# A two-layer DiT-like network on one core: the rotary sine product as one VectorE instruction with reversed blocks, and the column sums of layer 1's mixer gate moved from the attention phase to the convolution phase

## The chip, the cores and the metric

The kernel runs on 1 core of one Trainium2 chip. The metric is the device time of one execution in microseconds (us), the median of several runs. The core's engines are TensorE (PE in the profile, with its weight loads as PEld), VectorE (DVE), ScalarE (ACT), GpSimd (POOL) and SyncE (SP), which here only issues transfers. Each engine executes its own instructions in the order in which they were queued, and waits for the other engines through semaphores.

## What is computed

The reference works on 512 tokens of width 1024 (`x`), 256 context tokens and one conditioning vector. Cut to what bears on the change:

```python
def ada_params(cond, w_ada, b_ada):
    m = jax.nn.silu(cond) @ w_ada + b_ada          # 1024 x 6144: six vectors of 1024
    return jnp.split(m[..., None, :], 6, axis=-1)

def apply_rope(x, cos, sin):                        # head dim 64: four blocks of 16
    x1, x2, x3, x4 = jnp.split(x, 4, axis=-1)
    rot = jnp.concatenate([-x2, x1, -x4, x3], axis=-1)
    return x * cos[None, :, None, None, :] + rot * sin[None, :, None, None, :]
...
for l in range(DEPTH):                              # 2 layers
    sh_m, sc_m, g_m, sh_f, sc_f, g_f = ada_params(c, ada_w[l], ada_b[l])
    h = modulate(x, norm_mix[l], sh_m, sc_m)
    y = even_mixer(...) if l % 2 == 0 else odd_mixer(...)
    x = x + g_m * y
    x = x + g_f * ec_moe(modulate(x, norm_ffn[l], sh_f, sc_f), ...)
```

Layer 0's mixer is differential attention: 6 heads, each with two query and two key vectors of 64 and a value of 128. Queries and keys are normalised by their root mean square, multiplied by a gain, and rotated. Layer 1's mixer is a gated short convolution, `(bg * shortconv(cg * u)) @ w_out`. After each mixer comes a mixture of 16 experts in which each expert takes its 64 best tokens. The mixer's gate `g_m` of layer 1 is one of the 12 adaptive vectors; it multiplies the output of the convolution mixer, and nothing needs it earlier.

## The kernel before

**Phases.** By the time of the profile: a prologue (0 to 60 us), the attention heads (60 to 340), the attention's output projection with the first router (340 to 445), the first MoE (445 to 925), the convolution mixer (925 to 1136), and the second MoE (1136 to 1640). A scheduler of the tile framework puts each engine's instructions into one in-order queue, by priorities and by its own estimate of when operands are ready. A change in one instruction can therefore move others.

**Matrix products** outside the MoE run as three fp32r matmuls on operands split into a high and a low part (`mm3`). So each operand costs a rounding copy (`split`, ScalarE, line 244) and a subtraction (VectorE, line 245).

**An attention head.** While head h's scores, softmax and value products run, the projections of head h+1 are made, one token tile of 128 at a time, over six tiles (four of tokens, two of context). `proj_fin` (lines 391 to 424) ends a token tile. Of the 256 columns `j m d` (j: query or key, m: which of the two, d: 64), ScalarE makes the squares (L396) and the value's high part; VectorE makes the value's low part, the product with the cosine table `cosg` (L401), the product of the block-swapped columns with the sine table `sing` (L409: four instructions of 128x64, one for each b and j), the sum of squares (L417) and the sum of both products (L421); GpSimd makes the inverse root (L81, L82) and the scaled result `qk` (L423). TensorE then transposes `qk` (`proj_tr`, L440). Only the four token tiles have the sine product, so it occurs 6 x 4 = 24 times. Of one score tile, VectorE takes the row maximum (L463), ScalarE the exponential (L464), VectorE the reciprocal and its product with lambda (L470, L471), ScalarE scales one half (L472), VectorE combines both halves into `p` (L473), and TensorE transposes `p` (L486); the split of the transposed `p` gives `ah` and `al`.

**The tables** (`tables`, lines 312 to 322) are made once in the prologue: cosine and sine multiplied by the gains.

**The adaptive vectors** that are not needed at once are made in the gaps of other phases. One vector w of layer l takes four parts: `ada_part` (lines 158 to 170) loads two rows of a 1 MB slab, ScalarE scales one (L164, 128x1024), VectorE multiplies and adds (L168, two instructions of 128x512), and, except for the first part, GpSimd accumulates (L170, two instructions of 128x512). After four parts `ada_sum` (L172 to L177) sums the accumulator over the partitions with 8 matmuls on a column of ones (16 passes in the trace, `tr<-ones,ada`) and VectorE adds the bias (L177). `ada_steps` (L179) spreads the parts over a number of calls: NSTEP = 21 in the attention for 28 parts (layer 0's vectors 2 to 5 and layer 1's 0 to LW-1, with LW = 3), and 11 in the convolution for 12 parts (layer 1's vectors LW to 5).

**The ring.** The slabs, the heads' weights, the convolution's weights (`cw`) and the output projections' weights (`wo`) share a ring of RA = 4 buffers of 1 MB. A load is issued on SP's queue (L148 for most), and waits there until a buffer is free; behind it wait all later loads.

**The output projections** (`OutProj`, from L675) multiply each weight tile by the gate's row: VectorE `wg` (L699), ScalarE `woh` (L706), GpSimd `wol` (L707), then the matmuls `pj<-woh,zh` and its two companions, and VectorE adds the result to x (L721). The gate's row is built from the adaptive vector 2 by `gate_row` (L209 to L219: 8 matmuls `tr<-ident,ada`, two ScalarE copies). In the attention phase the output projection's object is made during the last head but one; in the convolution after the second of four column groups (`cp == 1`, L1212), when its first half is also run.

## Time and profile before

| | us |
|---|---|
| median of 3 runs | 1639.68 (1635.38 to 1641.67) |
| the profiled execution | 1642.39 |
| its span, first to last instruction | 1640.6 |
| outside the span | 1.8 |
| TensorE busy in the span | 1523.1 (93%) |
| VectorE busy | 694.3 (42%) |
| ScalarE busy | 385.8 (24%) |
| GpSimd busy | 222.7 (14%) |
| mean granted clock of TensorE | 0.969 |

The durations below come from the one profiled execution, whose time stands 2.7 us above the median. The share of an engine over the whole span says little, because the phases have different loads: VectorE has 42% of the span, but far more of the attention phase. So each stage is read by itself: first how busy its engines are, then what TensorE waited for in it, then the timeline around the longest of these waits.

### The profile page before, as it was taken

To read this page: it belongs to the slowest core of one execution; us is meant where nothing else is said; L and a number is where in the kernel's file an instruction comes from. 1 tells how busy PE (TensorE), PEld (TensorE's weight loads), DVE (VectorE), ACT (ScalarE), POOL (GpSimd) and SP (SyncE) were. 2 spreads that over 40 slices of the span, in tenths; PEclk is the share of its full clock that TensorE was granted. 3 is DMA by queue.
4 is the path that set the end of the run, shared out by engine and by line. 5 is a ranking of instruction groups with operands and counts; after the bars stand their busy time and mean duration, and the time that the engine had idled before them with its cause. 6 is when DMAs were issued, how large, how long until landed. Compare 5 with 4: busy or idle time off the path is not lost. (4 is left out here: it accounts for less than half of the span.)

```text
span 1640.6 us, 20218 instructions
## 1 busy us (share of the span) xinstructions
PE 1523.1 (93%) x8052; PEld 908.4 (55%) x8052; DVE 694.3 (42%) x1470; ACT 385.8 (24%) x745; POOL 222.7 (14%) x237
## 2 busy tenths in 40 slices
PE   5999999989689999999999899997899999999998
PEld 1988888868434434443443487886544444344343
DVE  3878888886512122212212668544221221221222
ACT  4545555553111000100100443222110010001010
POOL 0344445652000000000000024311000000000000
PEclk9899999989799999999999999998899999999999
DMA  9433534564698999999999456448899999999994
GB/s 347 156 103 129 177 132 154 170 214 189 253 380 315 409 409 409 409 409 409 409 408 395 145 180 227 133 154 321 307 365 398 409 409 409 409 409 408 409 405 184
DMA packets 162779, 494.82 MB, mean 302 GB/s; under 512 B 11749, under 2 KB 42878, under 8 KB 161662
## 3 DMA queue, kind: packets, MB, share of 16 engines
q1 hardware_dynamic: 161600, 491.23, 78.3%
q10 hardware_dynamic: 1086, 2.31, 0.4%
q8 instruction: 63, 1.03, 0.3%
q14 instruction: 30, 0.25, 0.0%
HBM read 491.41 MB, written 2.10 MB: 301 GB/s over the span
## 5 line engine op out<-in xcount | busy, mean ns | idle before, releaser
L965 PE MATMUL s<-we,xs 128*64 128x512 f32 x2048 | 450.8, 595 | 4.0 <-DVE xs L940 4.0
L965 PEld LDWEIGHTS s<-we,xs 128*64 128x64 f32 x2048 | 142.7, 137 | 281.8 <-issue 272.3
L965 PE MATMUL pj<-we,aT 128*64 128x512 f32 x896 | 206.1, 602 | 0.0
L66 PEld LDWEIGHTS tr<-oh,x 128*128 128x128 f32 x1024 | 122.4, 196 | 52.7 <-issue 52.7
L66 PE MATMUL tr<-oh,x 128*128 128x128 f32 x1024 | 134.7, 286 | 2.2 <-DVE oh L913 2.2
L940 DVE TENSOR_SCALAR xs<-tr,am,ada 128x128 f32<-128x128 f32 x64 | 26.1, 408 | 252.6 <-PE tr L66 252.6
L1043 DVE TENSOR_TENSOR act<-act,s 128x512 f32<-128x512 f32 x32 | 20.6, 684 | 251.9 <-PE s L965 251.8
L965 PEld LDWEIGHTS pj<-we,aT 128*64 128x64 f32 x896 | 59.7, 137 | 104.6 <-issue 99.2
L993 DVE TENSOR_TENSOR x<-x,tr 128x512 f32<-128x512 f32 x64 | 43.6, 684 | 142.7 <-PE tr L66 142.7
L170 POOL TENSOR_TENSOR ada<-ada,adaw 128x512 f32<-128x512 f32 x60 | 85.7, 1439 | 108.3 <-DVE adaw L168 48.7
L938 ACT ACTIVATE xs<-tr,ada,am 128x128 f32<-128x128 f32 x64 | 29.3, 457 | 296.2 <-DVE xs L940 296.2
L66 PE MATMUL pj<-whi,hh 128*128 128x384 f32 (+1 forms) x256 | 85.0, 333 | 0.4 <-ACT whi L244 0.4
L66 PE MATMUL pj<-wlo,hh 128*128 128x384 f32 (+1 forms) x256 | 83.8, 327 | 0.0
L66 PE MATMUL pj<-whi,hl 128*128 128x384 f32 (+1 forms) x256 | 82.7, 323 | 0.0
L1053 ACT COPY aT<-s 128x512 f32<-128x512 f32 x32 | 18.7, 585 | 222.2 <-PE s L1052 222.2
L1158 POOL TENSOR_TENSOR crs<-xsq 128x4 f32<-128x4 f32 x1 | 0.2, 200 | 503.1 <-ACT xT L1125 503.1
L1037 ACT ACTIVATE act<-s 128x512 f32<-128x512 f32 x32 | 17.4, 594 | 206.1 <-PE s L965 206.1
L66 PE MATMUL pj<-chh,clo 128*128 128x512 f32 x160 | 62.1, 390 | 0.9 <-DVE clo L245 0.9
L66 PE MATMUL pj<-chh,chi 128*128 128x512 f32 x160 | 62.4, 390 | 0.0
L66 PE MATMUL pj<-chl,chi 128*128 128x512 f32 x160 | 62.1, 389 | 0.0
L168 DVE SCALAR_TENSOR_TENSOR adaw<-adaw,cin 128x512 f32<-128x512 f32 x60 | 51.1, 865 | 23.2 <-ACT adaw L164 23.2
L707 POOL TENSOR_TENSOR wol<-wg,woh 128x512 fp32r<-128x512 f32 x32 | 45.2, 1426 | 99.9 <-ACT woh L706 94.9
(312 smaller groups left out, 2374.9 us busy)
## 6 DMA issues: line engine op xcount, KB each, us to landing
we<-in_moe_w_gate_dram SPq DMA_DIRECT2D x128, 1024.0 KB, 13.5
we<-in_moe_w_up_dram SPq DMA_DIRECT2D x128, 1024.0 KB, 16.9
we<-in_moe_w_down_dram SPq DMA_DIRECT2D x124, 1024.0 KB, 14.3
adaw<-in_ada_w_dram SPq DMA_DIRECT2D x48, 1024.0 KB, 5.3
cw<-in_conv_w_in_dram SPq DMA_DIRECT2D x12, 1024.0 KB, 5.4
wqk<-in_attn_w_in_dram SPq DMA_DIRECT2D x10, 512.0 KB
wo<-in_attn_w_out_dram SPq DMA_DIRECT2D x4, 1024.0 KB
we<-in_moe_w_down_dram SPq DMA_DIRECT2D x8, 512.0 KB
```

The lines of the kernel that those rows point to most:

```text
L66: return T.matmul(o, l, r, start=start, stop=stop, skip_group_check=True)
L168: V.scalar_tensor_tensor(o, s[:, 0, cs], cin[:, 0, j:j + 1], s[:, 1, cs], op0=ALU.mult, op1=ALU.add)
L170: G.tensor_tensor(acc[:, cs], acc[:, cs], o, op=ALU.add)
L707: G.tensor_tensor(lo, wg, hi.bitcast(F32), op=ALU.subtract)
L938: A.activation(o_, i_, AF.Identity, bias=sh[:, kk:kk + 1], scale=am[:, kk:kk + 1])
L940: V.tensor_scalar(o_, i_, am[:, kk:kk + 1], sh[:, kk:kk + 1], op0=ALU.mult, op1=ALU.add)
L965: pe(T.matmul(acc[hf][64 * j:64 * j + 64, :], lhs[:, 2 * kk + k, 64 * j:64 * j + 64], ws[j][:, k, hf * 512:hf * 512 + 512], start=kk == 0 ...
L993: V.tensor_tensor(x1[tt][:, cs], src[tt][:, cs], b, op=ALU.add)
L1037: A.activation(act[:, hf * 512:hf * 512 + 512], ga[hf], AF.Silu)
L1043: V.tensor_tensor(act[:, cs], act[:, cs], up[hf], op=ALU.mult)
L1053: A.copy(aT[:, 4 * k4:4 * k4 + 4, :].rearrange("p k c -> p (k c)"), b[k4])
L1158: G.tensor_tensor(rs, xsq[:, :, 0], xsq[:, :, 1], op=ALU.add)
```

## The change

There are two edits, and a consequence of the first.

1. The sine product of `proj_fin` is one instruction of 128x256. Its input is read with the two 16-blocks of each pair in reversed order (`src[:, :, ::-1, :]`), and its table has one row for every one of the 256 columns.
2. For that, the table `sing` is stored for both m (twice the size), and the gains are first copied with their 16-blocks swapped (`gx`, four copies of 128x2x16). The eight table products of 128x4x16 become four of 128x4x64.
3. LW goes from 3 to 2: layer 1's vector 2, the gate of its mixer, is made in the convolution phase. The attention keeps 24 parts and 6 column sums over the same 21 steps; the convolution gets 16 parts and 4 sums over the same 11 steps.

```diff
-        sing = tabs.tile([128, NT, 2, 64], F32, name="sing")
+        sing = tabs.tile([128, NT, 2, 2, 64], F32, name="sing")
+        gx_ = tabs.tile([128, 2, 64], F32, name="gx")
...
+            for b in range(4):
+                V.tensor_copy(gx_[:, :, 16 * b:16 * b + 16], gb[:, :, 16 * (b ^ 1):16 * (b ^ 1) + 16])
...
-                for b in range(4):
-                    V.tensor_tensor(sing[:, :, j, 16 * b:16 * b + 16], sing[:, :, 1, 16 * b:16 * b + 16],
-                                    gj[:, None, 16 * (b ^ 1):16 * (b ^ 1) + 16].to_broadcast([128, NT, 16]),
-                                    op=ALU.mult)
+                for m in range(2):
+                    V.tensor_tensor(sing[:, :, j, m, :], sing[:, :, 1, 1, :],
+                                    gx_[:, j, None, :].to_broadcast([128, NT, 64]), op=ALU.mult)
...
-                src = p[:, :256].rearrange("p (j m u b i) -> p j m u b i", j=2, m=2, u=2, b=2)
-                dst = t2.rearrange("p (j m u b i) -> p j m u b i", j=2, m=2, u=2, b=2)
-                tb_ = sing[:, tt].rearrange("p j (u b i) -> p j u b i", u=2, b=2)
-                for b in range(2):
-                    for j in range(2):
-                        V.tensor_tensor(dst[:, j, :, :, b, :], src[:, j, :, :, 1 - b, :],
-                                        tb_[:, j, None, :, b, :].to_broadcast([128, 2, 2, 16]),
-                                        op=ALU.mult)
+                src = p[:, :256].rearrange("p (g b i) -> p g b i", b=2, i=16)
+                V.tensor_tensor(t2.rearrange("p (g b i) -> p g b i", b=2, i=16), src[:, :, ::-1, :],
+                                sing[:, tt].rearrange("p j m (u b i) -> p (j m u) b i", u=2, b=2), op=ALU.mult)
...
-LW = 3
+LW = 2
```

What this does to the queues is shown at three places. The line numbers of the changed kernel differ by 2 or 3 (L699 is its L696, L396 its L398); `x2` behind a row means two instructions in a row.

The first is ScalarE's queue in head 0 (`adaw` is a slab being scaled; `p,su` an exponential; `qsq`, `qv`, `qk`, `ah` the steps of a tile's end and of the splits). Before:

```order
L464 ACTIVATE p,su<-s_902,nm 128x768
L464 ACTIVATE p,su<-s_903,nm 128x768
L396 ACTIVATE qsq<-pj 128x256
L244 CAST qv<-pj 128x128
L472 ACTIVATE p<-p,rc 128x768
L396 ACTIVATE qsq<-pj 128x256
L244 CAST qv<-pj 128x128
L164 ACTIVATE adaw<-adaw,cin 128x1024
L244 CAST qk<-tr 128x256
L244 CAST ah<-tr 128x3x128
L464 ACTIVATE p,su<-s_1041,nm 128x768
```

The same stretch in the changed kernel:

```order
L461 ACTIVATE p,su<-s_888,nm 128x768
L164 ACTIVATE adaw<-adaw,cin 128x1024
L461 ACTIVATE p,su<-s_889,nm 128x768
L398 ACTIVATE qsq<-pj 128x256
L244 CAST qv<-pj 128x128
L469 ACTIVATE p<-p,rc 128x768
L398 ACTIVATE qsq<-pj 128x256
L244 CAST qv<-pj 128x128
L244 CAST qk<-tr 128x256
L244 CAST ah<-tr 128x3x128
L461 ACTIVATE p,su<-s_1021,nm 128x768
```

The slab's scaling has moved from ahead of the split `qk` to between the two exponentials.

The second is the start of the last head, VectorE (`rc` is the softmax's reciprocal and its product, `amc` a modulation row that the convolution needs, `wg` the gated output weight). Before:

```order
L417 TENSOR_REDUCE qss<-qsq 128x2
L177 TENSOR_TENSOR ada_82<-tr,pcol 128x8
L168 SCALAR_TENSOR_TENSOR ada<-adaw,cin 128x512 x2
L470 RECIPROCAL rc<-su 128x2
L168 SCALAR_TENSOR_TENSOR adaw<-adaw,cin 128x512
L471 TENSOR_TENSOR rc<-rc,lam 128x1
L238 SCALAR_TENSOR_TENSOR amc<-ada_82,pcol 128x8
L699 TENSOR_TENSOR wg<-wo,gate_3643 128x512 x2
L473 SCALAR_TENSOR_TENSOR p<-p,rc 128x768
```

The same in the changed kernel:

```order
L414 TENSOR_REDUCE qss<-qsq 128x2
L467 RECIPROCAL rc<-su 128x2
L468 TENSOR_TENSOR rc<-rc,lam 128x1
L696 TENSOR_TENSOR wg<-wo,gate_3535 128x512 x2
L470 SCALAR_TENSOR_TENSOR p<-p,rc 128x768
```

Three multiply-adds of a slab, a vector's bias and `amc` no longer stand ahead of `p`. On GpSimd four accumulations (`ada`) no longer stand there ahead of the first `wol`; two stand earlier, among the last tile's steps.

The third is GpSimd's queue in the convolution phase. Before:

```order
L1158 TENSOR_TENSOR crs<-xsq 128x4
L81 TENSOR_SCALAR crs<-crs 128x4
L82 TENSOR_TENSOR crs<-crs,nhalf 128x4
L170 TENSOR_TENSOR ada<-ada,adaw 128x512 x12
L707 TENSOR_TENSOR wol<-wg,woh 128x512 x8
L170 TENSOR_TENSOR ada<-ada,adaw 128x512 x6
L707 TENSOR_TENSOR wol<-wg,woh 128x512 x8
```

The same in the changed kernel:

```order
L170 TENSOR_TENSOR ada<-ada,adaw 128x512 x12
L704 TENSOR_TENSOR wol<-wg,woh 128x512 x3
L170 TENSOR_TENSOR ada<-ada,adaw 128x512
L704 TENSOR_TENSOR wol<-wg,woh 128x512 x2
L170 TENSOR_TENSOR ada<-ada,adaw 128x512
L704 TENSOR_TENSOR wol<-wg,woh 128x512
L170 TENSOR_TENSOR ada<-ada,adaw 128x512 x2
L704 TENSOR_TENSOR wol<-wg,woh 128x512 x2
L170 TENSOR_TENSOR ada<-ada,adaw 128x512 x8
L704 TENSOR_TENSOR wol<-wg,woh 128x512 x8
```

Four accumulations now stand between the `wol` of the first half of the output projection. On VectorE there, one multiply-add of a slab stands ahead of the first gated weight `wg` and three between the first seven of them, where before one stood between the first six (and two weight splits `clo`, which are now behind).

## Rows read from the trace of the kernel before

**Rows 1.** Windows: us, busy us (instructions) PE, PEld, DVE, ACT, POOL; clock, DMA share, GB/s.

```profile
60.00:340.00 280.00, 259.66 (x1733) 230.90 (x1733) 232.41 (x551) 157.19 (x339) 136.87 (x160) 0.96 0.45 148
...
445.00:925.00 480.00, 462.49 (x2338) 204.28 (x2339) 107.97 (x234) 48.23 (x90) 0.00 (x0) 1.00 0.97 381
925.00:1136.00 211.00, 204.11 (x932) 165.72 (x934) 128.77 (x198) 75.56 (x124) 52.84 (x41) 0.96 0.54 190
```

**Rows 2.** What TensorE waited for, 60 to 400: us in total, times, longest.

```profile
PE tr L440 <- POOL qk L423: 6.0, 5, 2.4
PE tr L66 <- DVE al L245: 4.0, 2, 3.3
PE tr L486 <- DVE p L473: 3.9, 4, 2.6
PE s L66 <- ACT qk L244: 3.1, 1, 3.1
```

**Rows 3.** The same view inside the first MoE, 460 to 885.

```profile
PE s L66 <- DVE x L993: 6.3, 14, 0.5
```

**Rows 4.** Timeline, VectorE, end of one token tile: start, us, operation, idle before.

```profile
90.63 0.40 DVE L401 TENSOR_TENSOR t<-pj,cosg 128x256 f32<-128x256 f32 x1
90.96 0.60 DVE L409 TENSOR_TENSOR t<-pj,sing 128x64 f32<-128x64 f32 x4
91.49 0.40 DVE L417 TENSOR_REDUCE qss<-qsq 128x4 f32<-128x256 f32 x1
```

**Rows 5.** GpSimd's accumulations, whole span: duration ns min/median/max.

```profile
L170 POOL TENSOR_TENSOR ada<-ada,adaw x60: 1263/1296/2334, 72.0 to 1044.9; 128x512 f32<-128x512 f32 x60
```

**Rows 6.** Page, DMA issues of the adaptive weights: count, KB, us to landing.

```profile
adaw<-in_ada_w_dram SPq DMA_DIRECT2D x48, 1024.0 KB, 5.3
```

**Rows 7.** Timeline, TensorE: one column sum of the adaptive vectors.

```profile
172.46 1.94 PE L66 MATMUL tr<-ones,ada 128*128 128x1 f32 x16
```

**Rows 8.** Timeline, head 0, ScalarE and TensorE.

```profile
105.00 1.15 ACT L164 ACTIVATE adaw<-adaw,cin 128x1024 f32<-128x1024 f32 x1 [4.38 <-DMA adaw<-in_ada_w_dram]
...
107.44 0.86 PE L486 MATMUL tr<-ident,p 128*128 128x128 f32 x3 [2.48 <-DVE al L245]
```

**Rows 9.** Timeline, VectorE at the start of the last head.

```profile
323.13 1.55 DVE L168 SCALAR_TENSOR_TENSOR ada<-adaw,cin 128x512 f32<-128x512 f32 x2
...
324.68 1.68 DVE L168 SCALAR_TENSOR_TENSOR adaw<-adaw,cin 128x512 f32<-128x512 f32 x1
326.28 1.21 DVE L471 TENSOR_TENSOR rc<-rc,lam 128x1 f32<-128x1 f32 x1
...
327.49 3.44 DVE L699 TENSOR_TENSOR wg<-wo,gate 128x512 f32<-128x512 f32 x2
330.85 1.00 DVE L473 SCALAR_TENSOR_TENSOR p<-p,rc 128x768 f32<-128x768 f32 x1
```

**Rows 10.** Timeline, GpSimd and TensorE there, and the window's clock.

```profile
324.10 6.28 POOL L170 TENSOR_TENSOR ada<-ada,adaw 128x512 f32<-128x512 f32 x4
...
328.83 0.61 PE L66 MATMUL s<-qk 64*128 64x256 f32 x3 [3.11 <-ACT qk L244]
332.00 1.51 PE L486 MATMUL tr<-ident,p 128*128 128x128 f32 x6 [2.56 <-DVE p L473]
...
329.00:337.00 8.00, 5.44 (x27) 4.29 (x28) 8.00 (x12) 5.78 (x11) 3.74 (x3) 0.57 1.02 393
```

**Rows 11.** What TensorE waited for in the convolution phase.

```profile
PE pj L66 <- POOL wol L707: 0.6, 2, 0.4
```

**Rows 12.** Timeline, GpSimd at the convolution's output projection.

```profile
1008.99 3.23 POOL L707 TENSOR_TENSOR wol<-wg,woh 128x512 fp32r<-128x512 f32 x2 [3.16 <-ACT woh L706]
```

**Rows 13.** Timeline, VectorE splitting a weight slab, and GpSimd over the first one.

```profile
983.28 5.77 DVE L245 TENSOR_TENSOR clo<-cw,chi 128x512 fp32r<-128x512 f32 x4
...
997.05 2.50 DVE L245 TENSOR_TENSOR clo<-cw,chi 128x512 fp32r<-128x512 f32 x4 [1.16 <-ACT chi L244]
...
982.93 4.97 POOL L170 TENSOR_TENSOR ada<-ada,adaw 128x512 f32<-128x512 f32 x3 [24.80 <-DVE ada L168]
```

More of the change, by code (lines that the diff above doesn't have):

```diff
@@ L304, in table_loads @@
             SP.dma_start(out=cosg[:, :, 1, :], in_=t["cos"].rearrange("(a p) d -> p a d", p=128))
-            SP.dma_start(out=sing[:, :, 1, :], in_=t["sin"].rearrange("(a p) d -> p a d", p=128))
+            SP.dma_start(out=sing[:, :, 1, 1, :], in_=t["sin"].rearrange("(a p) d -> p a d", p=128))
             SP.dma_start(out=gb[:, 0, :], in_=row(t["attn_q_norm"], 64))
```

## The prediction

> **What bounds the kernel now.** I read the windows of the phases first [rows 1]. In both MoE phases TensorE is the limit: in the first it is busy 462.49 of 480.00 us at full clock, and its longest kind of wait inside is for VectorE's addition to x, 6.3 us in 14 pieces of at most 0.5 [rows 3]. The change touches nothing there, so these phases only shift. The convolution phase is nearly as full: 204.11 of 211.00 us, with VectorE at 128.77 and GpSimd at 52.84. The attention is different: TensorE has 259.66 of 280.00 us, VectorE 232.41 and GpSimd 136.87. There 20 us of the span are free on TensorE, and the engine next to it is VectorE, at 83%.
>
> So the second view is what TensorE waited for in the attention [rows 2]. The four largest kinds make 17.0 us: for the scaled queries and keys `qk` from GpSimd 6.0 (5 waits), for `al` from VectorE 4.0 (2), for `p` from VectorE 3.9 (4), for `qk` from ScalarE 3.1 (1). Three of the four end a step that passes VectorE. A gain on VectorE can thus reach the end of the phase, but only through some ten places; elsewhere TensorE has other matmuls queued and the time is hidden. So the third view is the timeline around the largest of these places, two of which hold over half of the sum: head 0 at 104.6 to 107.4 [rows 8], and the start of the last head at 325 to 335 [rows 9, 10].
>
> **The change part by part.**
>
> *The sine product.* VectorE's starts are closer than its durations, since each instruction begins before the last one has drained, so I count from start to start [rows 4]: the four sine instructions take 91.49 - 90.96 = 0.53 us, the cosine product of the same 256 columns 90.96 - 90.63 = 0.33. The new instruction has the cosine's size and sources; no row shows a negative step. Its bounds are the cosine's 0.33 and, since nothing excludes a loss, 0.73: the split form's 0.53 and the same excess over the cosine, 0.20, once more. I take 0.33, the row that it is nearest to in shape. The saving is 0.20 us, times 24 tiles (6 heads, 4 token tiles) 4.8 us of VectorE, between -4.8 and 4.8. It has no term of its own in the sum; it counts through VectorE's total below.
>
> The Trainium skill (VectorE: DVE Perf Modes, The TRN2 errata) gives a PSUM-to-SBUF instruction 120 cycles plus its elements at 0.96 GHz: 767 ns for four of 64, 392 for one of 256, so by it an estimated 24 x 0.375 = 9.0 us of VectorE would go instead of 4.8. The trace has 0.53 us where the page has 0.77, and the measurement decides.
>
> *The moved vector, on VectorE and the others.* From the attention go four loads of 1 MB [rows 6], four ScalarE scalings of 1.15 [rows 8], eight VectorE multiply-adds of about 0.75 each (1.55 for two [rows 9]), six GpSimd accumulations of 1.30 [rows 5] and one column sum of 1.94 on TensorE [rows 7]. So VectorE loses 6.0 us and with the sine product 10.8 of its 232; GpSimd loses 7.8 of 137. The same amounts arrive in the convolution phase, where DMA has a share of 0.54 and ScalarE is busy 75.56 of 211 us [rows 1]. On SP's queue four loads now stand between those of the convolution's weights; one lands 5.3 us after its issue, so four take 21 us of transfer in a phase with some 97 us of it free. The vector's own sum stands 144 projection matmuls ahead of the gate row on TensorE's queue, so I let nothing wait for it.
>
> *The column sum on TensorE* is work of the bounding engine in both places: -1.94 in the attention, +1.94 in the convolution, net 0.
>
> *The last head's start.* VectorE's queue had two multiply-adds (1.55), then one of 1.68, ahead of the softmax's `rc`, which itself took 1.21 with GpSimd accumulating beside it for 6.28; then two `wg` of 1.72 each, then `p` [rows 9, 10]. ScalarE's queue waited for `rc`, and the `qk` split stood behind it: TensorE waited 3.11, then 2.56 for `p`, together 5.67. The multiply-adds and four accumulations are gone from this place. What is late next: the `qk` split needs GpSimd's scaling and two transposes, and `p` still has the two `wg` ahead of it, whose gate row doesn't come sooner. I take 4 of the 5.67. This wait was followed by half clock: 329 to 337 had a mean of 0.57 with TensorE busy 5.44 of 8.00 [rows 10], so most of it ran at the lower level, 1.2 GHz. If the wait goes, the fall may go, worth at most half of the 5.44 us, 2.7; I take 1. Together -5, between 0 and -8.4.
>
> *Head 0's scaling.* ScalarE stood 4.38 us for a slab's transfer at 105.00, with the `qk` split queued behind it; TensorE ran out of work and waited 2.48 [rows 8]. Now the scaling stands between two exponentials about ten us earlier, and its load is issued earlier because its ring buffer comes free earlier. If the slab is there, the 2.48 go, and 0.5 for the exponentials that were late behind it: I take -3. If it is not, the exponential behind it waits instead, and the gain is given back. Between 0 and -4.4, ScalarE's whole wait.
>
> *The other waits of the attention.* Of the 17.0 us [rows 2] 5.67 are spent above (head 0's 2.48 belongs to a fifth kind); some 11 are left, most of them behind VectorE or GpSimd. VectorE is relieved by 10.8 of 232, 5%, and the scheduler reorders all later steps, so signs differ. I take -2.5, between +6 (new waits of the size of those seen, two of 3) and -6 (half of what is left).
>
> *The tables.* Four more copies and four products of 256 in place of eight of 64: by the pitches of rows 4 VectorE gets at most 8 x 0.33 - 8 x 0.13 = 1.6 us more in the prologue, behind which TensorE runs the first head's projections; without that cover +1.6. I take 0.
>
> *The convolution's output projection.* Four accumulations of 1.30 now stand between the first eight `wol` on GpSimd, and three multiply-adds of 0.75 between the `wg` on VectorE. TensorE already waited there for `wol`, but only 0.6 us in two pieces [rows 11]. Two `wol` took 3.23 [rows 12], so eight take 13 us. Four accumulations lengthen that to 18, and only those ahead of a `wol` that TensorE is close to are felt. I take +1.5, between 0 and +5.2 (all four).
>
> The sum: -5 - 3 - 2.5 + 1.5 + 0 = -9.0 us. Against the profiled execution of 1642.39 (span 1640.6 and 1.8 around it) that is 1633.4. The profiled execution stands 2.7 above the median of the runs, 1639.68; the same difference from the median gives **1631 us**. No wait in the MoE takes the difference back, since TensorE bounds it at both ends of its work.
>
> **The rivals.**
>
> *The relief does not reach TensorE* (same time). The waits of rows 2 are ends of chains through ScalarE and GpSimd too, and a shorter VectorE step can end in the same wait with another name; the place at 105 can move to the exponential. For it: TensorE is 93% busy in the attention, and four fifths of VectorE's 10.8 us lie beside it. Against it: the 5.67 us at the last head come from instructions that are gone from there. Price: between a kept gain of 4 and the convolution's +1.5 to +3 alone, 1636 to 1642.
>
> *The convolution gives it back* (slower). GpSimd's accumulations and VectorE's splits slow one another: the same four splits `clo` took 5.77 us with GpSimd accumulating beside them and 2.50 without [rows 13]. If six more accumulations and their multiply-adds stretch the `wg`, `wol` chain and the weight splits at a time when TensorE has under 0.6 us of waits, TensorE waits for `wol`: 5.2 us of accumulations, twice that with the stretch, and the sum's own 1.94. It decides as soon as the sixth `wol` is later than TensorE's sixth tile. With half of the attention's gain lost: 1639.68 - 4 + 10 = about 1646.
> The Trainium skill (SBUF — State Buffer, Who interferes with whom) has this as a rule: a VectorE instruction with two SBUF inputs and a GpSimd instruction that reads SBUF exclude one another. The 5.77 against 2.50 agrees with it; it speaks against moving accumulations beside weight splits, and for taking them out of the attention.
>
> *More than the sum.* All of the half clock in the two places stays away, and half of the remaining waits go: -8.4 - 4.4 - 6 + 1.5 = -17.3, 1622.4. By the 9.0 us that the Trainium skill (VectorE: DVE Perf Modes, The TRN2 errata) gives for the sine product this would be the likelier.
>
> *The reversed blocks cost more than four instructions.* At the sine's 0.53 or above, the sine product brings nothing or loses; with 24 tiles each 0.2 us dearer VectorE gets 4.8 us more and keeps 1.2 of its relief: the last head's 4 us stay, the rest goes, and the convolution's +1.5 remains: about 1637, within the first rival's time.
>
> **How the numbers follow.** The forecast, -4 to -14 us: 0.47. No relief (with the dear reversal), -4 to +3: 0.22. The convolution gives back, +3 to +10: 0.18. More than the sum, below -14: 0.13. The measurement tells 0.5%, 8.2 us, from no change. The forecast's mean lies just beyond this bound: 0.29 of its 0.47 count as faster, and with 0.13 that is 0.42. Same: 0.18 of the forecast, 0.22, and 0.06 of the third case, 0.46. Slower: 0.12. The range leaves out the slow end of the second rival and the far end of the third: 1620 to 1645.
>
> **What the changed profile would show.** The sine product at about 0.40 us, once per tile; at 0.6 and more the reversal is dear. VectorE's busy time in the attention about 11 us lower. ScalarE without the 4.38 us at head 0, TensorE without the 3.11 and 2.56 at the last head's start and with the clock above 0.57 there; if waits of over 2 us stand near with ScalarE or GpSimd as releaser, the first rival is right. In the convolution, waits for `wol` of over 2 us in all, and a phase over 213 us long, speak for the second. The MoE phases should keep their lengths, 480 us for the first; a change of over 1 us there would be something that I have not seen.

## The result: slower by 0.7%

| | before | after |
|---|---|---|
| median of 6 runs each, us | 1638.04 (1633.38 to 1641.67) | 1648.96 (1646.74 to 1653.39) |
| ratio, with its 95% interval | | 1.0072 [1.0050, 1.0093] |
| the profiled execution, us | 1642.39 | 1648.29 |
| its span, us | 1640.6 | 1646.5 |
| mean granted clock of TensorE | 0.969 | 0.968 |

The forecast was 1631 us, between 1620 and 1645. The time went up by 10.9 us instead of down by 9, and lies outside the range. The phases tell where. First the windows of the changed kernel, with the columns of [rows 1].

```profile
60.00:340.00 280.00, 261.86 (x1728) 230.97 (x1727) 228.54 (x478) 155.83 (x338) 133.37 (x158) 0.96 0.41 139
445.00:925.00 480.00, 462.07 (x2342) 205.61 (x2342) 111.86 (x244) 51.03 (x97) 0.58 (x3) 1.00 0.97 381
925.00:1136.00 211.00, 199.27 (x885) 161.80 (x884) 135.83 (x191) 74.73 (x115) 63.73 (x43) 0.94 0.59 205
```

The MoE is as before: TensorE 462.07 busy of 480 us. VectorE has 73 instructions fewer in the attention's window, but only 3.9 us less busy time (232.41 before); in the convolution's it has 7.1 us more, and GpSimd 10.9 more. There TensorE is busy 4.8 us less than before and its clock fell from 0.96 to 0.94. So the convolution phase is where most of the time came from.

Fixed windows cut stages that have shifted. Below, and in all comparisons of stages that follow, a stage runs between two of TensorE's own instructions: the attention from head 0's first projection of context tokens (69.5 us in the kernel before) to the first transpose of the router's scores (423.9), so with the output projection; the convolution from its first projection (934.2) to the next router's first matmul (1133.6). "Waits" is the sum of TensorE's gaps of over 0.1 us; "half clock" is the time that the granted clock stood at 1.2 GHz instead of 2.4. A microsecond at half clock costs up to half a microsecond (at place 2 below the same 128x512 matmul starts every 0.42 us at half clock and every 0.23 at full). The first MoE, from its first expert matmul to the convolution, keeps its 489 us in every trace of this table, and what follows the convolution its 507.

| trace (us of the execution) | attention | its waits | its half clock | convolution | its waits | its half clock |
|---|---|---|---|---|---|---|
| before, the one predicted from (1642.39) | 354.4 | 29.1 | 29.7 | 199.4 | 3.5 | 16.4 |
| before, another execution (1634.62) | 347.2 | 27.4 | 16.0 | 199.7 | 3.9 | 16.4 |
| after (1648.29) | 350.4 | 27.0 | 26.6 | 209.6 | 9.4 | 22.9 |
| after, another execution (1654.30) | 357.7 | 29.3 | 40.1 | 209.8 | 9.4 | 23.1 |
| sine edit alone (1639.79) | 353.8 | 34.4 | 16.3 | 199.0 | 3.1 | 16.1 |
| sine edit alone, another (1642.79) | 357.4 | 34.5 | 25.5 | 196.2 | 4.1 | 6.8 |
| move alone (1644.94) | 349.9 | 27.5 | 25.7 | 206.7 | 9.2 | 13.7 |

Two things are in it before any experiment is read. The convolution is 10 us longer: 5.9 of waits, 1.9 of the moved column sum, and at most 3.3 from 6.5 us more at half clock. And the trace that I predicted from was an execution with 13.7 us more half clock in the attention than another of the same program: there the attention took 347.2 us, not 354.4. Against that one the attention has lost 3 us, and in its second execution 10.5. Half clock scatters in the convolution too: all kernels with `LW = 3` have the same queues there, and their nine traces took 194.3 to 199.7 us, with 3.4 to 16.4 at half clock. A difference of 5 us between two single traces of that stage shows nothing.

### The profile page after: what moved, and what is told of

It reads as the page before. It is cut to its first block, busy times and chain, and to the rows that moved or that the text cites. A ratio compares the mean times of both kernels' runs of the same rounds, so it can differ in the third digit from the quotient of the medians.

```text
span 1646.5 us, 20168 instructions
## 1 busy us (share of the span) xinstructions
PE 1525.2 (93%) x8052; PEld 907.9 (55%) x8052; DVE 701.4 (43%) x1398; ACT 387.5 (24%) x745; POOL 225.4 (14%) x237
## 3 DMA queue, kind: packets, MB, share of 16 engines
q10 hardware_dynamic: 1086, 2.31, 0.4%
## 5 line engine op out<-in xcount | busy, mean ns | idle before, releaser
L935 ACT ACTIVATE xs<-tr,ada,am 128x128 f32<-128x128 f32 x64 | 29.3, 457 | 295.7 <-DVE xs L937 295.7
L164 ACT ACTIVATE adaw<-adaw,cin 128x1024 f32<-128x1024 f32 x40 | 46.1, 1152 | 35.8 <-DMA adaw<-in_ada_w_dram 33.5
## 6 DMA issues: line engine op xcount, KB each, us to landing
we<-in_moe_w_down_dram SPq DMA_DIRECT2D x124, 1024.0 KB, 15.5
```

What stands on the lines that cost most here:

```text
L164: A.activation(s[:, 1, :], s[:, 1, :], AF.Copy, scale=cin[:, 0, j + 1:j + 2])
L935: A.activation(o_, i_, AF.Identity, bias=sh[:, kk:kk + 1], scale=am[:, kk:kk + 1])
```

## The profile after, place by place

**The sine product.** Timeline of VectorE at the end of a token tile, columns as in [rows 4].

```profile
64.07 0.41 DVE L403 TENSOR_TENSOR t<-s,cosg 128x256 f32<-128x256 f32 x1
64.41 0.41 DVE L407 TENSOR_TENSOR t<-s,sing 128x256 f32<-128x256 f32 x1
64.74 0.41 DVE L414 TENSOR_REDUCE qss<-qsq 128x4 f32<-128x256 f32 x1
```

One instruction, 0.33 us from its start to the next one's, where the four took 0.53. Reading the 16-blocks in reversed order costs nothing over the cosine product beside it. The Trainium skill (VectorE: DVE Perf Modes, The TRN2 errata) has a formula by which one would estimate 392 ns for it; the trace has a duration of 0.41, and a pitch of 0.33.

**Head 0.** ScalarE's queue (and, behind the dots, TensorE's) in the changed kernel.

```profile
78.88 0.37 ACT L244 CAST qk<-tr 128x256 fp32r<-128x256 f32 x1
83.35 1.15 ACT L164 ACTIVATE adaw<-adaw,cin 128x1024 f32<-128x1024 f32 x1 [4.10 <-DMA adaw<-in_ada_w_dram]
84.40 0.62 ACT L244 CAST qk<-tr 128x256 fp32r<-128x256 f32 x2
...
84.81 0.50 PE L66 MATMUL s<-qk 64*128 64x512 f32 x2 [2.04 <-ACT qk L244]
```

The wait of 4.38 at 105 us [rows 8] is gone from there, and an equal one, 4.10, has appeared at 79. An earlier slab's scaling now stands ahead of the `qk` split that ends head 0's projections, and the first scores wait for it. In this order the slab's load could not be earlier: SP issued it at 78.06, when GpSimd's accumulation at 76.75 to 78.04 had set its ring buffer free, and the landing took the 5.3 us of [rows 6]. Behind the wait the clock fell to a mean of 0.51 from 86 to 93:

```profile
86.00:93.00 7.00, 7.00 (x25) 5.87 (x24) 6.35 (x10) 1.87 (x4) 5.39 (x4) 0.51 0.38 116
```

At the same projection matmul (87.4 us in the kernel before, 92.0 here) TensorE is 4.7 us behind the kernel before. At 115 us 2.0 of this are left, or 3.6 against the other execution of before, since the kernel before pays for its own wait at 105. This place is in every trace that has the sine edit and the old pacing of the slabs.

**The last head's start**, TensorE, to be held against [rows 10].

```profile
329.05 0.33 PE L437 MATMUL tr<-ident,qk 128*128 128x128 f32 x1 [1.88 <-POOL qk L420]
329.84 0.62 PE L66 MATMUL s<-qk 64*128 64x256 f32 x3 [0.46 <-ACT qk L244]
...
333.20 0.50 PE L66 MATMUL pj<-woh,oh 128*128 128x512 f32 x1 [1.02 <-ACT woh L703]
```

The 3.11 and 2.56 have become 1.88, 0.46 and 1.02: the instructions ahead of it are gone, and the next in line, GpSimd's `qk`, is the end of the wait. It gained 2.3 us.

**What TensorE waited for**, attention (60 to 400), then convolution (930 to 1150); columns as in [rows 2].

```profile
PE tr L437 <- POOL qk L420: 7.2, 8, 1.9
PE tr L66 <- DVE al L245: 3.7, 3, 2.8
PE tr L483 <- DVE p L470: 2.7, 4, 0.9
PE s L66 <- ACT qk L244: 2.5, 2, 2.0
...
PE pj L66 <- POOL wol L704: 3.5, 3, 1.3
PE pj L66 <- DVE z L1194: 2.9, 1, 2.9
...
PE pj L66 <- ACT woh L703: 1.5, 2, 1.2
```

In the attention the four kinds that made 17.0 us now make 16.1; the share of GpSimd grew from 6.0 to 7.2. In the convolution, waits for `wol` went from 0.6 to 3.5, and those for `z` and `woh` are not among the seven longest kinds of before.

**Convolution, place 1: the first half of the output projection.** TensorE, then GpSimd.

```profile
1004.03 0.73 PE L66 MATMUL pj<-woh,zh 128*128 128x512 f32 x2 [1.19 <-ACT woh L703]
1005.74 0.50 PE L66 MATMUL pj<-wol,zh 128*128 128x512 f32 x1 [0.98 <-POOL wol L704]
...
1009.93 0.51 PE L66 MATMUL pj<-wol,zh 128*128 128x512 f32 x1 [1.23 <-POOL wol L704]
...
1012.85 0.79 PE L66 MATMUL pj<-wol,zh 128*128 128x512 f32 x1 [1.27 <-POOL wol L704]
...
1008.21 1.66 POOL L704 TENSOR_TENSOR wol<-wg,woh 128x512 fp32r<-128x512 f32 x1 [1.28 <-DVE adaw L168]
1009.83 1.28 POOL L170 TENSOR_TENSOR ada<-ada,adaw 128x512 f32<-128x512 f32 x1
1011.08 3.40 POOL L704 TENSOR_TENSOR wol<-wg,woh 128x512 fp32r<-128x512 f32 x2
1014.44 1.72 POOL L170 TENSOR_TENSOR ada<-ada,adaw 128x512 f32<-128x512 f32 x1
```

GpSimd has no slack here: the accumulation at 1009.83 stands ahead of a `wol` that TensorE then waits for until 1012.85. At 1008 GpSimd itself had waited. The profile names a multiply-add of VectorE, which does not feed `wol`; `woh`, which does, ended at the same 1008.14. It is a loop: a `wg` needs one of two buffers that an earlier `wol` frees, `woh` needs `wg`, and `wol` needs both. VectorE shows it from the other side:

```profile
1005.72 1.76 DVE L696 TENSOR_TENSOR wg<-wo,gate 128x512 f32<-128x512 f32 x1 [1.17 <-POOL wol L704]
...
1013.26 3.45 DVE L696 TENSOR_TENSOR wg<-wo,gate 128x512 f32<-128x512 f32 x2
...
1017.88 0.69 DVE L696 TENSOR_TENSOR wg<-wo,gate 128x512 f32<-128x512 f32 x1 [0.57 <-POOL wol L704]
```

With GpSimd idle beside it (1017.88) a `wg` takes 0.69 us; beside GpSimd's work it takes 1.7, and the accumulation at 1014.44 takes 1.72 where the median of all is 1.30 [rows 5]. The Trainium skill (SBUF — State Buffer, Who interferes with whom) says that a VectorE instruction with two inputs in SBUF and a GpSimd instruction that reads SBUF contend for a port that only one of them holds at a time; the trace agrees, at 1.0 us for a `wg` and 0.4 for an accumulation. TensorE's six gaps of 1003 to 1018 sum to 5.75 us; in the whole phase before there were 0.6 for `wol` [rows 11] and 1.5 for the gate's row. From the projections ahead of this stretch to those behind it TensorE loses 6.1 us against the kernel before, counted at the same matmuls: 1.8 by the column sum, 4.3 by the place itself.

**Convolution, place 2: the loads for the second half.** SP's queue, then VectorE and TensorE.

```profile
1073.63 0.37 SPq L148 DMA_DIRECT2D adaw<-in_ada_w_dram  x1
1076.48 0.37 SPq L148 DMA_DIRECT2D cw<-in_conv_w_in_dram  x1
1078.18 1.52 SPq L148 DMA_DIRECT2D wo<-in_conv_w_out_dram  x2
...
1097.62 2.35 DVE L696 TENSOR_TENSOR wg<-wo,gate 128x512 f32<-128x512 f32 x2
1099.89 0.68 DVE L1194 TENSOR_TENSOR z<-cg,pj 128x512 f32<-128x512 f32 x1
...
1100.62 0.80 PE L66 MATMUL pj<-chh,chi 128*128 128x512 f32 x1 [2.86 <-DVE z L1194]
```

In the kernel before SP issued the two loads of the output weights' second half at 1050.57 and 1065.68. Here four more slabs stand ahead of them in the ring, and they leave at 1078 and 1079. So all eight gated weights `wg` come in a crowd from 1086 to 1100, the convolution's own `z` at 1099.89 stands behind two of them, TensorE waits 2.86, and then works at half clock until 1106.6. Counted in the same way, this place cost 6.0 us; 1.6 of them come back right behind it, where the kernel before had its own stretch at half clock.

## The experiments

Ratios are to the kernel before, run beside it on the same chip, with 95% intervals. From one set of such runs to another the kernel before itself had medians of 1634.59 to 1638.04 us, 0.2% apart, so ratios of different sets are to be compared with that in mind.

### Which edit loses?

**The new tables with the four old sine instructions** (they read one of the two equal halves of the new table):

```diff
-                tb_ = sing[:, tt].rearrange("p j (u b i) -> p j u b i", u=2, b=2)
+                tb_ = sing[:, tt, :, 0].rearrange("p j (u b i) -> p j u b i", u=2, b=2)
```

> The kernel before with the larger sine table and its longer making in the prologue, and the four old sine instructions reading it. Its queues stand as before, but for some twenty rows. Theory (the new order behind the shorter sine product makes the loss): 0.999 to 1.002 of before, TensorE's waits of over 0.1 us in the attention 27 to 30 us. Rival (the tables delay the first head): 1.003 to 1.007.

Measured 1637.37, ratio 0.9999 [0.9985, 1.0013]. The tables cost nothing.

**The sine edit alone** (changed kernel, `LW = 3`).

> Only the sine product and its tables are changed; layer 1's mixer gate stays in the attention. Theory (the loss is the moved vector's, in the convolution phase): the convolution phase is as long as before, the attention is shorter by what 4.8 us less VectorE work brings to TensorE, 0 to 3 us, so 0.998 to 1.000 of the kernel before. Rival (the new order that a shorter sine product causes loses time in the attention): 1.001 to 1.004. A convolution phase that is longer here too, by more than 2 us, would end the theory.

Measured 1645.03, ratio 1.0070 [1.0053, 1.0087]: my theory fell. Fewer instructions on VectorE made the kernel slower, all of it in the attention, where the waits rose from 27.4 to 34.4 us. What ScalarE waited for there, 60 to 340, for the kernel before, then for the sine edit alone:

```profile
ACT adaw L164 <- DMA adaw<-in_ada_w_dram: 10.0, 5, 4.4
...
ACT adaw L164 <- DMA adaw<-in_ada_w_dram: 17.5, 12, 4.0
```

In the new order ScalarE stands at twelve slabs that have not landed instead of five. (In the second executions, below, it is 15.5 us at nine against 12.6 at seven.)

The relief itself did not arrive either. VectorE over the attention stage, before and with the sine edit alone, columns as in [rows 1]; then two of its groups, before and after: count, busy us, mean ns, idle before.

```profile
69.54:423.92 354.38, 325.14 (x2078) 280.50 (x2077) 283.46 (x628) 181.66 (x384) 162.85 (x179) 0.96 0.47 164
67.96:421.71 353.75, 319.27 (x2078) 274.12 (x2077) 287.90 (x561) 182.28 (x385) 165.50 (x179) 0.98 0.48 165
...
L245 DVE TENSOR_TENSOR ol<-oT,oh 128x512 fp32r<-128x512 f32 x7 | 5.7, 831 | 0.8 <-PE pj L66 0.4 <-ACT oh L244 0.3
L245 DVE TENSOR_TENSOR ol<-oT,oh 128x512 fp32r<-128x512 f32 x7 | 8.8, 1280 | 0.8 <-PE pj L66 0.4 <-ACT oh L244 0.3
...
L471 DVE TENSOR_TENSOR rc<-rc,lam 128x1 f32<-128x1 f32 x24 | 7.4, 309 | 0.4
L468 DVE TENSOR_TENSOR rc<-rc,lam 128x1 f32<-128x1 f32 x24 | 9.9, 413 | 0.5
```

The sine products take 9.0 us of this stage instead of 13.3, and yet VectorE is busy 287.90 us instead of 283.46 (287.55 and 282.28 in the second executions). Its other instructions stand at other places and last longer: `ol` (the low part of the attention's output) by 3.1 us, `rc` by 2.5, `p` by 1.9 (27.2 to 29.1). Beside `ol` GpSimd works for 7.7 us instead of 2.6. So the 4.3 us that the product gave were more than taken back on VectorE itself.

**The move alone** (kernel before, `LW = 2`).

> Only LW = 2: the four sine instructions stay. Theory (the move makes the loss): the convolution phase is about 10 us longer, the attention 0 to 4 us shorter, so 1.004 to 1.007 of the kernel before. Rival (the loss needs both edits, since each changes the order): under 1.002.

Measured 1644.70, ratio 1.0066 [1.0051, 1.0081]. The convolution has both places (waits 9.2 us; 7 us longer), with the same queues as in the changed kernel, and the attention has no gain against the second execution of before.

Each edit alone costs 0.7% in this set of runs, and both together 0.72%. They don't add: with both the attention's waits are 27.0 us, with the sine edit alone 34.4. That this is so because both reorder the attention is likely, and not shown.

### How much differs between executions?

One more profiled execution of each of three programs, nothing changed.

> The kernel before, once more, for a trace from the same chip as the next two. If the trace of before that the prediction was made from is a usual execution, TensorE reaches the first MoE within 1 us of the 441 us seen there. If that execution was a late one (its 1642.39 us stands above all others of this kernel), it does so 3 to 8 us earlier, and the gain of 4.1 us that the first comparison gave to the changed attention is not there.

> The kernel with the sine product alone, once more: its first profiled execution was the fastest of four (1639.79 against 1643.70 to 1647.12). If its loss lies in the attention, as the trace of the first execution allows, TensorE reaches the first MoE here 4 to 8 us later than in the trace of before taken with it; the convolution phase and both MoE phases are as long as in that one.

> The changed kernel, once more, beside the other two. Theory (two losses that don't add, since the sine product's order and the move act on the same places of the attention): the attention is 0 to 4 us later than before's, the convolution phase 8 to 10 us longer. Rival (the attention gained 4 us): it is 3 to 5 us earlier.

The times were 1634.62, 1642.79 and 1654.30; the stages are in the table above. The first expectation came: TensorE is at the router 7.9 us earlier than in the trace predicted from. The other two were too low: beside that execution of before the sine edit's attention is 10.2 us longer (4 to 8 expected), the changed kernel's 10.5 (0 to 4). The waits of one program agree within 2.3 us between executions, and the half clock in the attention differs by 9 to 14. That is the larger part of what scatters. The Trainium skill (TensorE: Matmul & The Clock Gate, What's actually happening) says that how long a kernel's start runs slow varies from run to run; here the same is seen in its middle.

### The convolution's two places

**Accumulations of the convolution phase on VectorE** (changed kernel; aimed at place 1).

```diff
-                G.tensor_tensor(acc[:, cs], acc[:, cs], o, op=ALU.add)
+                (V if l and w > 1 else G).tensor_tensor(acc[:, cs], acc[:, cs], o, op=ALU.add)
```

> The changed kernel, with the convolution phase's 24 accumulations of the adaptive vectors on VectorE (0.68 us each by the time of an addition of this size) instead of GpSimd (1.30 to 1.72). Theory A (GpSimd's accumulations, and VectorE and GpSimd slowing one another, delay the weights of the first half of the output projection): TensorE's 5.8 us of waits there fall to under 2, the kernel is 4 to 7 us faster than the changed one, 0.999 to 1.004 of before. Rival B (it is the order on the queues, multiply-adds ahead of the gated weights): VectorE has 24 x 0.68 = 16 us more in the same order, the waits stay or grow, 1.007 to 1.012. The second loss, at the end of the last column group, should stay under both.

Measured 1645.50, ratio 1.0060 [1.0040, 1.0081]. Neither theory A's time nor rival B's came. In that trace the convolution is 201.3 us long; `wol` waits are 1.2 instead of 3.5, and waits for VectorE's addition to x are up from 0.7 to 2.4:

```profile
PE pj L66 <- DVE x L718: 2.4, 2, 2.0
...
PE pj L66 <- DVE z L1194: 1.6, 1, 1.6
PE pj L66 <- POOL wol L704: 1.2, 2, 1.0
```

What left GpSimd arrived in part at VectorE: of the 4.3 us at place 1 about 2.6 remain. Place 2 was to stay, and shrank: the wait for `z` is 1.6 instead of 2.9, and TensorE loses 1.9 us there instead of 6.0. The rest of the shorter stage is 16 us less at half clock, which one trace cannot assign.

**The output weights' second half loaded a group earlier** (changed kernel; aimed at place 2).

```diff
+            if cp == 2:
+                wo.pre[2] = wo.load(1, 0)
+                wo.pre[3] = wo.load(1, 1)
...
-            s = self.load(g, half)
+            s = self.pre.pop(i) if i in self.pre else self.load(g, half)
```

> The changed kernel, with the loads of the output projection's second half asked for after the third column group instead of after the fourth, so that they stand ahead of six adaptive slabs' loads fewer on SP's queue. Theory C (the second loss, 5.8 us at 1095 to 1107, comes from these loads standing behind the four added slabs in the ring): the wait of 2.86 us for z and the half clock behind it go, 3 to 6 us faster than the changed kernel, 1.003 to 1.005 of before. Rival (VectorE's and GpSimd's work there is the cause, whenever the loads land): the wait stays, 1.006 to 1.009. If the early loads hold ring buffers that the convolution's own weights need, TensorE waits for those instead, and the time is above the changed kernel's.

Measured 1643.42, ratio 1.0055 [1.0040, 1.0070]. The wait for `z` is gone from the list, the timeline shows no wait of TensorE between 1088 and 1110, and the 6.0 us of place 2 have not been lost there (TensorE stands 2.1 us behind the kernel before ahead of it and 2.2 behind it). The phase is 203.8 us long, 5.8 less than with the change. So the late load was the cause of place 2. The kernel's time, just above the expected range, is not clear of the changed kernel's 1.0072 by the intervals.

**Both cures on the move alone.**

> The kernel before with LW = 2, the convolution phase's accumulations on VectorE, and the second half's output weights asked for after the third column group. Theory (the convolution loses 1.94 us by the column sum, the rest by the two collisions): the convolution phase from its first matmul to the router's is 200 to 203 us long against 206.7 with the move alone, and the time 1.000 to 1.003 of before. Rival (each cure brings its own waits): 1.004 to 1.008.

Measured 1641.24, ratio 1.0031 [1.0020, 1.0042]: half of the move's loss is gone. The convolution is 203.1 us long, its waits 5.7; of the 3.5 us that are left against before 1.9 are the column sum.

### The attention: work or order?

**The sine edit alone with 72 fills more** (in the program, three memsets of 128x1 behind each sine product; in the trace they are elsewhere).

```diff
+                pad = sm.tile([128, 1], F32, tag="pad", name="pad", bufs=1)
+                for _ in range(3):
+                    V.memset(pad, 0.0)
```

> The sine product alone, with three small fills of 128x1 on VectorE behind each one (0.06 us each by the trace, so about 0.18 of the 0.20 us saved is put back). The order on every engine stays that of the sine product alone. Theory (order, not the amount of VectorE's work): the same time as the sine product alone, 1.004 to 1.008 of before, TensorE's waits in the attention 33 to 36 us. Rival (VectorE's work bounds the attention and the saving is real, only hidden by noise): 2 to 5 us slower than the sine product alone, 1.007 to 1.011.

Measured 1641.91, ratio 1.0040 [1.0024, 1.0056]; the attention's waits are 35.9 us, and the slab still stops ScalarE at 78 us, for 5.16. But the fills, which depend on nothing, were all placed in the prologue, and none behind a sine product (count, duration ns min/median/max, first and last start):

```profile
L411 DVE MEMSET pad<- x72: 59/59/59, 1.4 to 23.6; 128x1 f32 x72
```

So no work was put back into the attention, and the run can't tell the amount of VectorE's work from its order. What it is: the sine edit alone once more, since apart from the fills every engine's queue is the same. The waits repeat (34.4, 34.5, 35.9). The loss was 0.70% in one set of runs and 0.40% in the other.

**One more vector in the attention** (kernel before, `LW = 4`), a step in the other direction.

> The kernel before with one vector more in the attention instead of one less (LW = 4). Theory (what the convolution loses with a vector more it does not win back with one less, since before it had few waits to lose: 3.5 to 3.9 us): convolution 1.9 to 4 us shorter, attention 2 to 5 us longer, 0.999 to 1.003 of before. Rival (each vector is worth 7 to 10 us in the convolution): 0.996 or less.

Measured 1650.16, ratio 1.0089 [1.0071, 1.0106]. I expected no change, and was wrong: the attention takes 367.3 us (waits 35.0, half clock 36.0). ScalarE's wait for slabs in it:

```profile
ACT adaw L164 <- DMA adaw<-in_ada_w_dram: 21.7, 11, 4.2
```

The convolution took 194.1 us, with none at half clock; with its old queues it took 194.3 in another trace, so no gain is shown. So the attention loses 13 us or more with a vector put in, and gains nothing that can be seen with one taken out (349.9 against 347.2 and 354.4). Whether the number of vectors does this or where the scheduler then puts each scaling, this run doesn't separate.

**All parts paced a little later** (sine edit alone; each part is made a little later; the last of the 28 parts, one of layer 1's gate vector, is left out).

```diff
-            while n < len(todo) and n * steps < (step + 1) * len(todo):
+            while n < len(todo) and n * steps < (step + (steps < 20)) * len(todo) + 1:
```

> The sine product alone, with each part of the attention's adaptive vectors one step later (the first step takes one part instead of two). ScalarE's scaling of a slab then no longer stands ahead of the first head's split of its scaled queries. Theory (in the kernels with the new sine product the wait for a slab moved from 105 to 83 us, where TensorE has less work queued: 2.0 us of wait and some 3 us of half clock): 3 to 6 us less than the sine product alone, 1.000 to 1.004 of before. Rival (that wait is one of many, and the others take its place): 1.005 to 1.009.

Measured 1644.38, ratio 1.0060 [1.0039, 1.0081]. The wait at 79 us is gone, but ScalarE stands 3.07 us for a slab at 91 and 3.52 at 103, and GpSimd's `qk` makes TensorE wait 9.3 us. The time is the rival's, but this didn't separate the theories: it moves all parts and so makes a third order.

**One dependency** (sine edit alone): the fourth slab's scaling may not start before the last `qk` split of head 0's projections. All else stands in the same order, but for the subtraction that follows the split.

```diff
+        m = A.activation(s[:, 1, :], s[:, 1, :], AF.Copy, scale=cin[:, 0, j + 1:j + 2])
+        pin["n"] = pin.get("n", 0) + 1
+        if pin["n"] == PINN:
+            tc.add_manual_dep(m.ins, pin["after"].ins.name, SYNC, reason="behind the split")
```

> The sine product alone, with the fourth slab's scaling on ScalarE made to stand behind the last split of the first head's queries and keys instead of ahead of it. All other queues stay as with the sine product alone. Theory (this place makes 4.7 us of the loss, 2.1 of wait and 2.7 of half clock): TensorE's wait of 2.1 us for qk at 82 us is gone, and the time is 3 to 5 us less than the sine product alone, 1.001 to 1.004 of before. Rival (the exponentials behind the scaling are late instead, and TensorE waits for them): no more than 1 us less, 1.004 to 1.007.

Measured 1640.86, ratio 1.0017 [1.0001, 1.0033]. ScalarE there:

```profile
82.96 0.37 ACT L249 CAST qk<-tr 128x256 fp32r<-128x256 f32 x1 [1.38 <-PE tr L442]
84.85 1.15 ACT L166 ACTIVATE adaw<-adaw,cin 128x1024 f32<-128x1024 f32 x1 [1.52 <-DMA adaw<-in_ada_w_dram]
```

The split now waits for TensorE, not for the slab; the slab's wait is short and stops nobody. At the projection matmul where the sine edit alone is 4.5 us behind the kernel before, this one is level with it, and the half clock behind the place (84 to 91 us) is gone. TensorE's waits in the attention fell from 34.4 to 29.3, ScalarE's for slabs from 17.5 to 10.8, though the later order is the same. By the medians one instruction's place in ScalarE's queue was worth 0.5 of 0.7%, or 0.2 of the 0.4% that the same queues cost with the fills; these are sets of runs on different chips. The one trace can't confirm it: its attention is 356.0 us long, no shorter than the sine edit's 353.8 and 357.4, with 28.2 at half clock.

### All cures, and a better kernel

**The changed kernel with all three cures.**

> The changed kernel with all three cures: the slab's scaling behind the split, the convolution's accumulations on VectorE, the second half's output weights asked for after the third column group. Theory (the three places are most of the loss): 1.000 to 1.004 of before, 5 to 11 us faster than the changed kernel. Rival (the changed order has many small waits in the attention, and these stay): 1.004 to 1.008. Below 0.998 it would beat the kernel before.

Measured 1639.33, ratio 1.0017 [1.0001, 1.0033]. By the medians three quarters of the loss are gone with the three places. The rest, 0.17%, is some 2.8 us, and the convolution is still 3.5 longer; no gain came of the 10.8 us that VectorE was to save.

**The kernel before, with the same rule at its own wait at 105 us**: the fifth slab's scaling behind the next `qk` split of head 1 (`PINN = {5: (1, 0)}`, the same dependency).

> The kernel before, with the fifth slab's scaling (the one that ScalarE waited for at 105 us) made to stand behind the split of the next head's queries and keys; all other queues as before but for a few rows. Theory: the wait for al at 104 us (1.2 us in one trace of before, 2.5 in the other, the latter followed by 3.4 us of half clock) goes, and the time falls by 1 to 4 us, 0.9975 to 0.9995 of before. Rival (the scaling delays an exponential by as much, or the time went into the next wait): 0.9995 to 1.001.

Measured 1632.46, against 1637.39 of before: ratio 0.9974 [0.9959, 0.9989], faster than both kernels. ScalarE at the place of [rows 8]:

```profile
103.49 0.36 ACT L249 CAST qk<-tr 128x256 fp32r<-128x256 f32 x1
103.94 1.15 ACT L166 ACTIVATE adaw<-adaw,cin 128x1024 f32<-128x1024 f32 x1
104.99 0.46 ACT L249 CAST ah<-tr 128x384 fp32r<-128x384 f32 x1
```

The 4.38 are gone, and the slab is there when its turn comes. TensorE's wait of 2.48 (1.15 in the other execution of before) is 0.24. Only ScalarE's, VectorE's and TensorE's order around this place differs from before. The gain is the size of what the baseline moves between sets of runs, but both kernels were run side by side here, and the interval leaves out 1.

## Why the prediction was wrong

In the sum the attention was to be 12.4 us shorter, column sum included, and the convolution 3.4 longer. The attention is 4.0 shorter than in the trace predicted from and 3.2 longer than in another execution of before; the convolution is 10.2 longer. So two steps failed: the relief of the attention, and the price of the convolution.

*The sine product* (0.33 us taken, 4.8 saved): right to the hundredth. What failed is the step from there to the end. I let it count "through VectorE's total", as relief of a busy engine. With the sine edit alone that total did not fall: VectorE is busy 4.4 us longer in the attention, since other instructions last longer at their new places, and the kernel is 0.4 to 0.7% slower. With both edits VectorE's busy time there is 276.22 us, 7.2 or 6.1 below before, not 10.8. Whether relief without a new order would have reached TensorE no run shows.

*Head 0's scaling* (-3 taken, "if it is not [there] ... the gain is given back", down to 0): the step failed. For the scaling that I looked at it held: it runs at 99.36 us between the exponentials, without a wait. I did not look at the one before it, which had moved ahead of a `qk` split. The bound of 0 was wrong too: that place cost 4.7 us, and past the old one 2.0 to 3.6 of loss are left instead of 3 of gain.

*The other waits* (-2.5, between +6 and -6): wrong in sign with the sine edit alone (all waits of the attention 34.4 against 27.4 and 29.1); with both edits all waits are what they were (27.0 and 29.3), though the last head's start gained 2.3. "Signs differ" was right; the -2.5 rested on the relief.

*The last head's start* (-4 of 5.67, and -1 of clock): mechanism right, size off. The waits fell by 2.3, since GpSimd's `qk` was the next in line, as the text said it could be. Of the clock 325 to 340 shows 1.00 in one execution of after, and 0.81 in the other: nothing to count on.

*The convolution* (+1.5 beside the sum's 1.94): mis-sized by about 7 us, and this made the sign. Place 1 was seen and priced low, 1.5 us for 4.3: I counted accumulations ahead of a `wol`, and not the loop through `wg` and `woh`, in which the two engines also slow one another. Place 2, 4.4 us net, was not seen. "Four take 21 us of transfer in a phase with some 97 us of it free" answers whether the loads have room, and the question was where they stand: in a ring that issues in order, a fourth vector's slabs hold back the output weights by up to 28 us (1050.57 to 1078.18). With these weights asked for a group earlier the place was gone.

*The rivals.* The second, with 0.18, was the nearest: its place 1, its releaser and its sign are in the trace, and it gave 1646. Its sign of "waits for `wol` of over 2 us in all" came (3.5). It held no second place, and left half of an attention gain that wasn't there.

*The base.* The sum of -9 was taken from an execution whose attention was 7.2 us longer than another's, mostly by half clock. The terms with clock in them (-1 at the last head, part of the -3) priced something that ordinary executions have less of. It made no sign, but I could have known: 1642.39 stood above the highest of the runs shown, 1641.67.

*Right*: the tables at nothing (0.9999), the column sum's +1.94 and -1.94, the MoE phases unchanged.

*Open.* Why half clock in the attention differs by up to 14 us between executions of one program was not tried. What the last 0.17% consists of isn't settled; the column sum's new place and the remainder of place 1 are in the same phase. Why the sine edit costs less in the attention when the move is there too is not shown, and neither is which of its waits, beyond head 0's, make the rest of its loss.

## What to carry to other kernels

Where in-order queues mix urgent work with filler, ask of every filler instruction that waits for a transfer what stands right behind it, and place it with one dependency behind the urgent instruction: here that gave 0.3% to the old kernel and took 0.2 to 0.5% from the one with the sine edit. Work taken from an engine that is 83% busy is worth what the waits behind it are worth, and the reordering that comes with it may cost more; look in the trace whether the engine's busy time fell at all. Look there too where a control's extra work ended up, before you read its time. Before you move a load, follow the ring's order to the next load that is needed on time, not the bandwidth; and take a second trace before you price anything that hangs on the clock.

## What was not expected of the hardware

The granted clock of one and the same program differed by execution: 16.0 or 29.7 us at 1.2 GHz in the attention of before, 26.6 or 40.1 after, with nearly the same waits. The reversed blocks cost nothing (0.33 us pitch, 0.41 duration, both the cosine's). Beside GpSimd's work VectorE pays more than GpSimd: a `wg` took 0.69 us by itself and 1.7 beside it, an accumulation 1.28 or 1.72. Even the product `rc` of one column, 0.16 us by itself, took 1.21 beside an accumulation [rows 9, 10].
